# Moving the second set of modulation vectors from TensorE to VectorE, returning the memory of two tables, and new figures in the emitter of a two-layer diffusion backbone

## The chip, the cores and the metric

The kernel runs on one core of one Trainium2 chip. The metric is the device time of one execution in microseconds (us). Three executions of the kernel before took 1827.73, 1830.83 and 1835.16 us; their median is 1830.83 us. The profile shown here is of a further execution, of 1827.55 us.

## What is computed

The reference is a backbone of two layers over 2048 latent tokens of 1024 channels (x) with 256 context tokens. Both layers are modulated by vectors that come out of a conditioning vector c:

```python
s_lat = jax.nn.silu(c)
shift, scale, gate = jnp.split((s_lat @ ada_w[i] + ada_b[i])[:, None, :], 3, axis=-1)
a = rmsnorm(h, norm_g[i]) * (1.0 + scale) + shift
...
h = h + gate * y
```

Layer 0 (even) projects `a` to queries, keys, values, two gate paths and the input u of a state layer (S5: 32 groups of 16 channels, 64 complex states per group and direction, scanned forward and backward). Window attention (128 tokens to either side, 256 context tokens, a sink per head) and the state layer (followed by a gated linear unit, GLU) are joined by one output projection. Layer 1 (odd) is a pooling mixer: an input projection with gate, centred means over 3, 5, 9 and 17 tokens, a mixing matrix that is folded into the input weights, and an output projection. A final RMSNorm ends it.

For each layer `ada_w[i]` is 1024 by 3072. This text calls layer 0's shift and scale (for latents and context) the first set, and the other four vectors, layer 0's gate and layer 1's shift, scale and gate, the second set: 4096 sums of 1024 products each, 16.8 MB of weights. The second set is read for the first time by the output projection of layer 0.

## The kernel before, in words

Large products run on TensorE as three fp32r products of high and low halves (`split`, `products`), with the channel dimension on the partitions and 512 tokens as moving columns; smaller ones (state layer, tables, modulation) run on plain fp32 operands, for which the trace has two records per matmul.

**The emitter.** The program is not written in its final order. Each piece of work is a Python generator (`t_ada1`, `t_u`, `t_gen` and so on). An emitter (`Threads`) keeps a clock per engine from a cost for every instruction (`issue`, line 176; DMAs in `dma`, line 219), always resumes the generator whose next step is due first (`run`, line 243), and so writes one static order for each engine's queue. On the chip each engine works through its queue in that order and waits on semaphores; one SyncE queue issues all DMAs. The cost figures thus decide the order of all five queues, and for some elementwise steps (`lighter`, line 514) whether VectorE or GpSimd gets them. Bias terms hold back two of the generators.

**Memory.** All SBUF is given out by hand in words per partition (`Mem`, `Buf`, `Ring`): `core_f` of 16192 words and `x2` of 12384 words for fp32, `core_r` of 4096 and `x3` of 16384 for fp32r, and `x1` of 4128, which is reopened as fp32 or fp32r between stages. A generator that finds no room (`need`, line 404) waits until something is freed.

**Stages around the change.**
- *The u stage.* `t_load` loads x in five parts (the context, then quarters 2, 3, 0, 1) of eight rows of 128 channels, with at most 14 rows held. `t_stat`, `t_rstd`, `t_scale` and `t_apply` make the norm and the modulated, split rows; `rstd` (line 894) has two sets of small matmuls and a reciprocal (L492). `t_u` multiplies each quarter by four weight tiles for u (for the context also keys and values) and stores u to DRAM. Beside it run `t_s5par` (state parameters, GpSimd), then `t_etab` (four parts of a rotation table, stored to e_scr, in a work space `s5w` of 3328 words and `pw` of 512), `t_ltab` and `t_lags` (tables of the output side, stored to o_scr and r_scr).
- *The flag "x1f".* When `t_u` has ended, `t_main` takes six stage buffers of 512 words and two rope tables of 1024, reopens `x1` as fp32 and sets "x1f". The state layer waits for it: `t_s5u` and `t_s5e` (loads), `t_gen` (input tables, from PGr and PGi, two tables of 512 words), `t_s5` (input products), `t_rot` (rotation and scan, VectorE) and `t_s5out` (output products, z stored to z_scr). Beside it `t_main` runs the projection to keys, values, queries and gates (56 tiles of 24 products on TensorE).
- *Attention.* `t_qk` starts when the state layer has stored z and the gate stage is far enough; `t_exp`, `t_norm`, `t_pv` follow unit by unit (32 units), with `t_fold` and `t_glu` beside them.
- *Output projection of layer 0 (`t_out0`).* It waits for "fold" (the flag of `t_fold`), takes a weight stream (`Weights`: raw ring of 2 by 1024 words in `core_f`, split ring in `core_r`, which GLU holds until its end), then xin 3, hst 3, sqt 2 and r1 4 buffers of 512 words, all in `core_f`; then it waits for "gate0". Layer 1 follows.

**What the change touches.** `t_ada1` (lines 630 to 672) makes the second set. It starts when the first set has freed its buffers ("ada_free"), takes a ring of three buffers of 1024 words and a row buffer, and loads `adaM` in 32 loads of 512 KB. For each of eight blocks of 512 outputs it runs eight fp32 matmuls whose stationary operand is silu(c) (128 by 2) and whose moving operand is 512 columns of weights, copies the 2 by 512 result to SBUF (ScalarE), turns it onto partitions by four transposes of 2 by 128, and adds the bias on VectorE. It shares TensorE's queue with `t_u`.

`t_gen` (lines 1328 to 1353) frees PGr and PGi only if the flag "gen_end" already stands:

```python
        if "gen_end" in flags:
            PGr.free()
            PGi.free()
        flags.add("gen_end")
```

One `t_gen` runs in this kernel, so the flag never stands there, and the two tables are held to the end.

Helper lines of the profile: L464 `tt` (tensor_tensor), L475 `stt`, L483 `ttr` (tensor_tensor_reduce, a custom VectorE instruction and a read of its accumulator), L488 scan, L492 reciprocal, L498 `act`, L504 `mm`, L508 `transpose`, L512 `dma`. The name x_f stands for x1 or x2 opened as fp32, x_r for x1, x2 or x3 as fp32r.

Of the kernel before, what the change touches and what calls it, by code (L numbers as in the profile page):

```python
# [16 lines left out]
D = 1024  # L17
# [16 lines left out]
DMAF = 1.1  # L34
# [4 lines left out]
NADA1 = 3  # L39
# [78 lines left out]
class Threads:  # L118
# [8 lines left out]
    DMA_LAG, HOP, DELAY, CLOCK = 1.6, 0.1, 0.12, 3.4133  # L127

    def __init__(self):
        self.bias = {"t_fold": BF, "t_glu": BG}  # L130
        self.clock, self.spans, self.live, self.fresh = {}, {}, [], []
        self.now = self.end = self.stored = 0.0
        self.port = {"dve": [], "pool": []}
        self.lands = []
        self.window, self.busy, self.fast = 0, 0.0, False
# [40 lines left out]
    def issue(self, engine, cost, outs, ins, port=False):  # L176
# [29 lines left out]
        for x in outs:  # L206
            x[0] = f + self.HOP
        self.end = max(self.end, f)

# [9 lines left out]
    def dma(self, o, i, store):  # L219
# [10 lines left out]
        self.clock["dma"] = max(s + 0.5, self.clock.get("dma", 0.0)) + DMAF * n / run / 16 * (0.006 + run * 0.000194)  # L230
        f = self.clock["dma"] + self.DMA_LAG
        self.lands.append(max([f] + self.lands[-1:]))
# [57 lines left out]
def body(ctx: ExitStack, tc: tile.TileContext, I, out):  # L290
# [168 lines left out]
    def use(e, c, outs, *ins, port=False):  # L459
        th.issue(ename[id(e)], c, outs, [x for x in ins if isinstance(x, bass.AP)], port)  # L460
# [45 lines left out]
    def transpose(o, i, ident):  # L506
        use(TE, 0.22, [o], i)
        return TE.transpose(o, i, ident)  # L508
# [120 lines left out]

    def t_ada1():  # L630

        yield from wait("ada_free")
        ring = yield from need(lambda: Ring(NADA1, 2, 512))
        row = yield from need(lambda: Buf(512))
        w = {}

        def load(i):
            if i < 32:
                w[i] = ring.next()
                dma(w[i], I["adaM"][i // 4, i % 4].rearrange("p (k n) -> p k n", k=2))  # L640

        for i in range(NADA1):
            load(i)
        for blk in range(8):
            b = yield from get_bank()
            ps = bank(b)
            for i in range(4):
                yield from arrived(w[4 * blk + i])
                t_ = w.pop(4 * blk + i)
                for k in range(2):  # L650
                    mm(ps[0:2], silu.f[:, 2 * i + k], t_[:, k], i == k == 0, i == 3 and k == 1)
                yield
                load(4 * blk + i + NADA1)
            r = row.f[0:2]
            act(r, ps[0:2], AF.Copy, scale=0.5)
            yield
            for j in range(4):
                transpose(ps[:, 2 * j:2 * j + 2], r[:, 128 * j:128 * (j + 1)], K["ident"][0:2, 0:2])
            yield
            got = ps[:, 0:8:2]  # L660
            vec, sl = (gate0, sh1, gs1, gate1)[blk // 2], slice(4 * (blk % 2), 4 * (blk % 2) + 4)
            add = (K["b0"][:, 16:24], K["b1"][:, 0:8], K["b1"][:, 8:16], K["b1"][:, 16:24])[blk // 2]
            tt(V, vec[:, sl], got, add[:, sl], OP.add)
            put_bank(b)
            if blk // 2 == 2:
                stt(gs1[:, sl], gs1[:, sl], 1.0, K["g1"][:, sl], OP.add, OP.mult)
            if blk == 1:
                flags.add("gate0")
            yield
        flags.add("ada1")  # L670
        for b in (ring, row):
            b.free()
# [655 lines left out]
    def t_gen(e):  # L1328
# [20 lines left out]
        if "gen_end" in flags:  # L1349
            PGr.free()  # L1350
            PGi.free()
# [1232 lines left out]
def _layout(i):  # L2584
# [38 lines left out]
    def tiles(w):  # L2623
# [17 lines left out]
adaM=ac(np.concatenate([np.asarray(i["ada_w"][0])[:, 2 * D:], np.asarray(i["ada_w"][1])], axis=1)  # L2641
                .reshape(4, 2, 128, 8, 512).transpose(3, 0, 2, 1, 4).reshape(8, 4, 128, -1)),
# [26 lines left out]
```

## Time and profile before

| | before |
|---|---|
| median of three runs (lowest to highest) | 1830.83 us (1827.73 to 1835.16) |
| profiled execution, its own time | 1827.55 us |
| its span, first to last instruction | 1825.8 us |
| mean granted TensorE clock | 0.979 |
| busy: TensorE (PE), VectorE (DVE), ScalarE (ACT), GpSimd (POOL) | 1717.7, 1283.4, 828.3, 594.7 us |
| moved by DMA, mean rate | 286.16 MB, 157 GB/s |
| share of PE in the chain that ended last | 74% |

The profile is one execution, with times in us from the first instruction. "Busy" is the time in which an engine had an instruction in work. Windows give the busy time of each engine in a stretch, with the granted TensorE clock and the busy share of the 16 DMA engines. The chain of waits goes back from the last instruction to whatever released each step. A group line gives engine, line, operation, tiles, shape and count, then the busy time, the mean of one in ns, and the idle time of the engine just before, with what ended it.

### The profile page before, as it was taken

Reading aid. Unit: us, or ns where it says so; the run is one execution under the profiler, and the core shown is the slowest. Engines: PE = TensorE matmul, PEld = TensorE weight load, DVE = VectorE, ACT = ScalarE, POOL = GpSimd, SP = SyncE. Lnnn points to the kernel's source line nnn. Section 1 sums busy time; section 2 is a strip of 40 time slices with the busy share of each in tenths; the row PEclk is TensorE's granted clock in tenths of the full one; section 3 lists DMA queues with packets and bytes.
Section 4 is the critical chain, followed back from the end, with each engine's and each line's share of the span. In section 5 each row is a group of like instructions: output and inputs, shape, how many; then the busy total and the mean of one; then the engine's idle time right before and its main releaser. Section 6 shows DMA issues by size and latency. Waiting matters only on the chain.

```text
span 1825.8 us, 24990 instructions
## 1 busy us (share of the span) xinstructions
PE 1717.7 (94%) x8488; PEld 1366.8 (75%) x8488; DVE 1283.4 (70%) x2150; ACT 828.3 (45%) x1689; POOL 594.7 (33%) x722
## 2 busy tenths in 40 slices
PE   6899998979998999988897999999999999999997
PEld 1654465758887887777775788888888888888897
DVE  3569764997878945777888879687656764666634
ACT  4545431335444433687677766544322332222311
POOL 4887655663244410435363534230000000000000
PEclk9999998989998999999999999999999999999998
DMA  7777565235665456465855446687211263441332
GB/s 287 221 239 219 162 172 177 97 123 172 193 216 155 156 162 180 137 185 140 238 159 160 114 137 182 203 254 231 87 58 46 75 201 127 141 135 48 105 87 86
DMA packets 226000, 286.16 MB, mean 157 GB/s; under 512 B 60112, under 2 KB 155088, under 8 KB 224848
## 3 DMA queue, kind: packets, MB, share of 16 engines
q1 hardware_dynamic: 225872, 284.56, 51.6%
q8 instruction: 67, 1.10, 0.2%
q14 instruction: 61, 0.50, 0.1%
HBM read 204.60 MB, written 79.89 MB: 156 GB/s over the span
## 4 chain that ended last, share of the span: by engine, by line
PE 74%; DVE 9%; DMA 6%; ACT 4%; POOL 3%; issue 3%; SPq 1%; DVEq 0%; ACTq 0%; POOLq 0%
PE psum L504 71%; PE psum L508 3%; DVE x_r L464 2%; DVE core_f L464 2%; DVE x_f L464 2%; POOL core_f L464 2%; ACT x_f L498 2%; ACT x_r L498 1%; SPq L512 1%; POOL core_f L469 1%; DMA x_f<-u_scr 1%; DVE core_f L475 1%; DMA core_f<-a_scr 1%; DMA core_f<-sg_scr 1%; DMA core_f<-in_s5p 1%
## 5 line engine op out<-in xcount | busy, mean ns | idle before, releaser
L504 PE MATMUL psum<-x_r,core_r 128*128 128x512 f32 (+3 forms) x4536 | 1080.5, 393 | 5.7 <-ACT core_f L498 1.5
L504 PEld LDWEIGHTS psum<-x_r,core_r 128*128 128x128 f32 x4536 | 841.5, 189 | 199.1 <-issue 20.4
L504 PE MATMUL psum<-x_r 128*128 128x256 f32 (+3 forms) x1808 | 372.8, 348 | 13.7 <-DVE x_r L464 4.5
L464 DVE TENSOR_TENSOR core_f<-core_f 128x512 f32<-128x512 f32 (+20 forms) x443 | 301.3, 692 | 49.4 <-ACT core_f L498 22.0
L504 PEld LDWEIGHTS psum<-x_r 128*128 128x128 f32 x1808 | 284.0, 195 | 47.9 <-issue 12.9
L464 POOL TENSOR_TENSOR core_f<-core_f 128x32 f32<-128x32 f32 (+8 forms) x321 | 235.5, 748 | 178.9 <-ACT core_f L498 57.3
L464 DVE TENSOR_TENSOR core_r<-core_f,core_r 128x512 fp32r<-128x512 f32 (+1 forms) x182 | 135.1, 742 | 170.8 <-ACT core_r L498 168.1
L498 ACT ACTIVATE core_r<-core_f 128x512 fp32r<-128x512 f32 (+1 forms) x224 | 141.0, 632 | 220.6 <-PE psum L504 129.3
L498 ACT ACTIVATE core_f<-psum 128x512 f32<-128x512 f32 (+2 forms) x217 | 116.0, 535 | 257.9 <-PE psum L504 238.9
L498 ACT ACTIVATE x_r<-core_f 128x512 fp32r<-128x512 f32 (+5 forms) x173 | 127.0, 745 | 99.6 <-DVE core_f L475 69.0
L470 POOL TENSOR_SCALAR x_f<-x_f,core_f 128x640 f32<-128x640 f32 (+1 forms) x128 | 131.1, 1037 | 105.4 <-DVE core_f L492 66.7
L508 PE MATMUL psum<-core_f,x_f 128*128 128x128 f32 (+1 forms) x792 | 123.0, 279 | 30.5 <-DVE x_r L464 24.4
L464 DVE TENSOR_TENSOR x_r<-psum,x_r 128x512 fp32r<-128x512 f32 (+2 forms) x174 | 112.1, 649 | 48.9 <-ACT x_r L498 45.1
L508 PEld LDWEIGHTS psum<-core_f,x_f 128*128 128x128 f32 (+1 forms) x792 | 96.2, 144 | 62.8 <-DVE x_r L464 31.0
L498 ACT ACTIVATE x_f<-x_f,core_f 128x640 f32<-128x640 f32 (+2 forms) x155 | 123.5, 798 | 36.1 <-DVE core_f L475 32.4
L475 DVE SCALAR_TENSOR_TENSOR core_f<-core_f 128x512 f32<-128x512 f32 (+12 forms) x162 | 122.0, 762 | 20.8 <-DMA core_f<-h_scr 12.2
L498 ACT ACTIVATE core_f<-core_f 64x32 f32<-64x32 f32 (+7 forms) x224 | 83.4, 372 | 113.7 <-DVE core_f L475 94.9
L479 POOL COPY core_f<-core_f 128x16 f32<-128x16 f32 (+2 forms) x35 | 8.7, 262 | 369.1 <-DVE core_f L475 293.3
L464 POOL TENSOR_TENSOR core_r<-core_f,core_r 128x512 fp32r<-128x512 f32 x42 | 61.8, 1475 | 203.6 <-ACT core_r L498 203.6
L498 ACT ACTIVATE x_f<-psum 128x512 f32<-128x512 f32 (+5 forms) x187 | 77.7, 447 | 93.3 <-PE psum L504 80.7
L464 DVE TENSOR_TENSOR x_f<-x_f 128x512 f32<-128x512 f32 (+5 forms) x155 | 116.5, 780 | 3.4 <-ACT x_f L498 1.6
L498 ACT ACTIVATE x_r<-psum 128x512 fp32r<-128x512 f32 (+2 forms) x174 | 97.1, 562 | 48.1 <-PE psum L504 42.7
(64 smaller groups left out, 1314.0 us busy)
## 6 DMA issues: line engine op xcount, KB each, us to landing
core_f<-in_wo SPq DMA_DIRECT2D x48, 512.0 KB
core_f<-in_w SPq DMA_DIRECT2D x42, 512.0 KB
x_f<-in_adaM SPq DMA_DIRECT2D x32, 512.0 KB
core_f<-in_xT SPq DMA_DIRECT2D x45, 256.0 KB
x_f<-in_adaN SPq DMA_DIRECT2D x8, 1024.0 KB
o_scr<-core_f SPq DMA_DIRECT2D x32, 256.0 KB
x_f<-o_scr SPq DMA_DIRECT2D x16, 512.0 KB
sg_scr<-core_f SPq DMA_DIRECT2D x32, 256.0 KB
```

Source lines behind the costliest of these rows:

```text
L464: return e.tensor_tensor(o, a, b, op=op)
L469: return e.tensor_scalar(o, a, s1, None, op0=op0)
L470: return e.tensor_scalar(o, a, s1, s2, op0=op0, op1=op1)
L475: return V.scalar_tensor_tensor(o, a, s, b, op0=op0, op1=op1)
L479: return e.tensor_copy(o, a)
L498: return S.activation(o, i, f, **kw)
L504: return TE.matmul(o, w, x, start=start, stop=stop)
L508: return TE.transpose(o, i, ident)
L512: return nc.sync.dma_start(o, i)
```

## The change

The diff has three parts.

1. `t_ada1` is rewritten. It now waits for "x1f". It takes a buffer of 1024 words with silu(c) on every partition (c is loaded once with a partition broadcast, and ScalarE and VectorE make its silu) and a ring of three rows of 1024 words. The weights come transposed (`adaT`, 4096 rows of 1024): each of 32 loads of 512 KB brings 128 outputs onto the partitions, and one `ttr` of 128 by 1024 on VectorE multiplies them by silu(c) and sums along the row into one column of `ada`, a new buffer of 32 words that is kept to the end. Its order is gate0, shift1, scale1, gate1; the bias additions follow ("gate0" after eight rows, "ada1" at the end). TensorE, PSUM and the transposes are no longer used.
2. `t_gen` frees PGr and PGi at its end, without a condition: 1024 words of `core_f`.
3. The emitter's figures: a transpose costs 0.11 instead of 0.22; a result of TensorE is ready 0.17 later (DRAIN); the clocks of VectorE, ScalarE and GpSimd stand 0.08, 0.095 and 0.035 before the end of their last instruction (AHEAD); and DMA time is kept on 16 rings by the number of rings that a transfer's shape uses, with new constants, where it was one clock, and transfers may land out of order.

```diff
-DMAF = 1.1
+DMAF = 1.0
...
-NADA1 = 3
...
-    DMA_LAG, HOP, DELAY, CLOCK = 1.6, 0.1, 0.12, 3.4133
+    DMA_LAG, HOP, DELAY, CLOCK, DRAIN = 1.6, 0.1, 0.12, 3.4133, 0.17
+    AHEAD = {"dve": 0.08, "act": 0.095, "pool": 0.035}
...
-        self.lands = []
+        self.lands, self.rings = [], [0.0] * 16
...
-            x[0] = f + self.HOP
+            x[0] = f + self.HOP + (self.DRAIN if engine == "pe" else 0.0)
         self.end = max(self.end, f)
+        self.clock[engine] = f - self.AHEAD.get(engine, 0.0)
...
-        self.clock["dma"] = max(s + 0.5, self.clock.get("dma", 0.0)) + DMAF * n / run / 16 * (0.006 + run * 0.000194)
+        a, b = (next((int(d[1]) for d in x.ap if int(d[1]) > 1), 1) for x in (o, i))
+        k = max(k for k in range(1, 17) if a % k == b % k == 0)
+        for j in range(k):
+            self.rings[j] = max(s + 0.5, self.rings[j]) + n / run / k * (0.008 + run * 0.000152 * DMAF)
+        self.clock["dma"] = max(self.rings[:k])
         f = self.clock["dma"] + self.DMA_LAG
-        self.lands.append(max([f] + self.lands[-1:]))
+        self.lands.append(f)
...
     def transpose(o, i, ident):
-        use(TE, 0.22, [o], i)
+        use(TE, 0.11, [o], i)
...
+    ada = Buf(32, top=True)
+
     def t_ada1():
 
-        yield from wait("ada_free")
-        ring = yield from need(lambda: Ring(NADA1, 2, 512))
-        row = yield from need(lambda: Buf(512))
+        yield from wait("x1f")
+        silu_c = yield from need(lambda: Buf(D))
+        ring = yield from need(lambda: Ring(3, D))
+        dma(silu_c.f, I["c"].partition_broadcast(128))
         w = {}
 
         def load(i):
             if i < 32:
                 w[i] = ring.next()
-                dma(w[i], I["adaM"][i // 4, i % 4].rearrange("p (k n) -> p k n", k=2))
...
+                dma(w[i], I["adaT"][128 * i:128 * (i + 1), :])
+
+        yield LOAD
+        t_ = ring.next()
+        act(t_, silu_c.f, AF.Tanh, scale=0.5)
+        yield
+        stt(silu_c.f, t_, 1.0, silu_c.f, OP.add, OP.mult)
+        load(0)
+        load(1)
+        for i in range(32):
+            load(i + 2)
+            yield from arrived(w[i])
+            x = w.pop(i)
+            ttr(x, x, silu_c.f, OP.mult, OP.add, 0.0, ada.f[:, i:i + 1], scale=0.5)
+            yield
+            if i == 7:
+                tt(V, gate0, ada.f[:, 0:8], K["b0"][:, 16:24], OP.add)
                 flags.add("gate0")
...
         flags.add("ada1")
-        for b in (ring, row):
+        yield
+        for b in (ring, silu_c):
             b.free()
...
-        if "gen_end" in flags:
-            PGr.free()
-            PGi.free()
+        PGr.free()
+        PGi.free()
         flags.add("gen_end")
```

More of the change, by code (lines that the diff above doesn't have):

```diff
@@ L639, in load @@
                 w[i] = ring.next()
-                dma(w[i], I["adaM"][i // 4, i % 4].rearrange("p (k n) -> p k n", k=2))
[L642 to L655, printed above, removed]
-            yield
[L657 to L667, printed above, removed]
+                dma(w[i], I["adaT"][128 * i:128 * (i + 1), :])
[11 more added lines that the diff above has]
+            ttr(x, x, silu_c.f, OP.mult, OP.add, 0.0, ada.f[:, i:i + 1], scale=0.5)
+            yield
+            if i == 7:
+                tt(V, gate0, ada.f[:, 0:8], K["b0"][:, 16:24], OP.add)
                 flags.add("gate0")
-            yield
+        tt(V, sh1, ada.f[:, 8:16], K["b1"][:, 0:8], OP.add)
+        tt(V, gs1, ada.f[:, 16:24], K["b1"][:, 8:16], OP.add)
+        stt(gs1, gs1, 1.0, K["g1"], OP.add, OP.mult)
+        tt(V, gate1, ada.f[:, 24:32], K["b1"][:, 16:24], OP.add)
         flags.add("ada1")
-        for b in (ring, row):
+        yield
+        for b in (ring, silu_c):
             b.free()
@@ L2640, in _layout @@
         adaN=ac(np.asarray(i["ada_w"][0])[:, :2 * D].reshape(8, 128, 2, 4, 256).transpose(3, 1, 0, 2, 4).reshape(4, 128, -1)),
-adaM=ac(np.concatenate([np.asarray(i["ada_w"][0])[:, 2 * D:], np.asarray(i["ada_w"][1])], axis=1)
-                .reshape(4, 2, 128, 8, 512).transpose(3, 0, 2, 1, 4).reshape(8, 4, 128, -1)),
+adaT=ac(np.concatenate([np.asarray(i["ada_w"][0])[:, 2 * D:].T, np.asarray(i["ada_w"][1]).T])),
         w0=tiles(np.asarray(i["even_w_in"][0])[:, order]),
```

## The prediction

> **What bounds the kernel now.** I read the page first, then the engines' busy time by stage, TensorE's order of work in the u stage, and last who waits for whom. The page and the windows (columns: window, its length, then busy us and count for PE, PEld, DVE, ACT and POOL, granted clock, DMA share, GB/s):
>
> ```profile
> span 1825.8 us, 24990 instructions
> ...
> PE 1717.7 (94%) x8488; PEld 1366.8 (75%) x8488; DVE 1283.4 (70%) x2150; ACT 828.3 (45%) x1689; POOL 594.7 (33%) x722
> ```
> ```profile
> 50.00:130.00 80.00, 74.04 (x338) 46.35 (x338) 43.66 (x73) 43.57 (x71) 70.73 (x165) 0.98 0.77 241
> 130.00:260.00 130.00, 126.52 (x464) 64.60 (x463) 106.48 (x160) 59.02 (x131) 81.67 (x97) 1.00 0.61 175
> 260.00:311.00 51.00, 42.64 (x162) 30.59 (x163) 23.24 (x33) 8.91 (x27) 32.25 (x46) 0.90 0.61 187
> 311.00:400.00 89.00, 75.41 (x355) 56.11 (x354) 80.37 (x107) 28.07 (x82) 58.14 (x48) 0.94 0.30 100
> 400.00:664.00 264.00, 254.90 (x1475) 222.18 (x1473) 216.31 (x342) 123.51 (x278) 98.96 (x74) 0.98 0.58 176
> 664.00:757.00 93.00, 90.42 (x446) 74.91 (x445) 52.65 (x122) 44.72 (x97) 13.99 (x15) 1.00 0.54 159
> 757.00:950.00 193.00, 170.40 (x969) 143.97 (x968) 156.72 (x293) 141.42 (x297) 91.44 (x74) 0.95 0.66 183
> 950.00:1025.00 75.00, 59.57 (x331) 47.09 (x330) 64.18 (x141) 55.21 (x125) 35.44 (x37) 0.93 0.51 137
> 1025.00:1175.00 150.00, 148.49 (x804) 125.12 (x804) 117.94 (x240) 98.30 (x208) 56.07 (x52) 1.00 0.55 165
> 1175.00:1800.00 625.00, 625.00 (x2937) 531.35 (x2936) 389.43 (x553) 200.24 (x328) 31.49 (x48) 1.00 0.40 123
> ```
>
> TensorE bounds the kernel: 1717.7 of 1825.8 us, and from 1025 to 1800 it is idle for 1.5 us. So a saving counts if it takes work from TensorE's queue where that queue is the limit, or fills one of its gaps. Between 50 and 1175 the gaps come to 82.6 us; the largest for its length is 950 to 1025, 15.4 of 75 us. VectorE is the second engine: 106.5 of 130 us late in the u stage, 80.4 of 89 us at the start of the state layer.
>
> **What is removed from TensorE.** The group of the old matmuls (with the first set's), the loads, and TensorE in order of time (start, length, what; in brackets the idle time before):
>
> ```profile
> L504 PE MATMUL psum<-x_f,core_f 128*2 128x512 f32 x192 | 90.2, 602 | 2.8 <-DMA x_f<-in_adaM 1.6 <-DMA x_f<-in_adaN 1.2
> ```
> ```profile
> L512 SPq DMA_DIRECT2D x_f<-in_adaM x32: 327/382/737, 52.1 to 223.2; - x32
> ```
> ```profile
> 203.47 1.88 PE L504 MATMUL psum<-x_f,core_f 128*2 128x512 f32 x4
> 205.28 1.65 PE L504 MATMUL psum<-x_r,core_r 128*128 128x512 f32 x6
> ...
> 211.30 0.41 PE L508 MATMUL psum<-core_f,x_f 2*128 2x2 f32 x4
> 211.64 1.65 PE L504 MATMUL psum<-x_r,core_r 128*128 128x512 f32 x6
> ...
> 214.27 7.13 PE L504 MATMUL psum<-x_r,core_r 128*128 128x512 f32 x30
> ...
> 226.89 0.96 PE L504 MATMUL psum<-x_r,core_r 128*128 128x512 f32 x3
> ...
> 238.27 0.50 PE L504 MATMUL psum<-x_r,core_r 128*128 128x512 f32 x1 [0.95 <-ACT x_r L498]
> 239.00 1.18 PE L504 MATMUL psum<-x_r,core_r 128*128 128x512 f32 x4 [0.23 <-DVE x_r L464]
> ```
>
> The 192 records are two per matmul: 32 matmuls of the first set, 64 of the second. One of the 32 loads feeds two matmuls, four records, and holds TensorE from 203.47 to 205.28, 1.81 us: 32 x 1.81 = 57.9 us. The eight times four transposes hold it from 211.30 to 211.64 each, 8 x 0.34 = 2.7 us. So **60.6 us** leave TensorE's queue, all between 52 and 237 us, where it is busy for 200.6 of 210 us (50 to 260).
>
> How much of that shortens the u stage? At most 60.6 us, if TensorE alone sets its end. The last quarter says that it doesn't:
>
> ```profile
> L512 SPq DMA_DIRECT2D x_f<-in_xT x19: 328/384/1447, 27.7 to 159.4; - x19
> ```
> ```profile
> 188.41 0.17 DVE L492 RECIPROCAL x_f<-x_f 128x4 f32<-128x4 f32 x1
> ```
> ```profile
> ACT x_f L498 <- PE psum L504: 24.0, 12, 3.5
> ```
>
> The last row of x is requested at 159.4, its quarter's norm is at the reciprocal at 188.4, and TensorE takes the rows one at a time (three records each: the 226.89 row) until 238.3, when it waits for ScalarE and VectorE. The other tiles of that quarter need 4 x 24 products x 0.238 us (7.13 us for 30) = 22.8 us in all. So from 159 to 239 rows are made hardly faster than they are used. TensorE enters this chain through the matmuls of the norm, which queue behind modulation and u products (between 128 and 240 ScalarE's work on x_f alone waits 24.0 us for TensorE), and by its own pace before. If only the norm's queueing goes, some 10 us are won; if all, 60.6. I take **30 us**, half: before about 170 us TensorE does not wait for rows, after it does. The end of the u stage, and "x1f" with it, comes near 230 instead of 260.
>
> A price here is the clock. At 84% busy (260 to 311) the granted clock is 0.90; the thinner u stage would be like that. Its products left, some 100 us, would take up to 11 us more, most of it inside waits; I take +2. [...]
>
> **What is added to VectorE.** No row shows a `ttr` of 128x1024 from SBUF. Near rows:
>
> ```profile
> L483 DVE DVE_READ_ACCUMULATOR2_ANT core_f<- x144: 71/82/92, 709.3 to 1142.3; 128x1 f32 x144
> L483 DVE CUSTOM_DVE_ANT_0 x_f<-psum,x_f x128: 392/815/826, 708.9 to 1141.5; 128x640 f32<-128x640 f32 x112, 128x256 f32<-128x256 f32 x16
> ```
> ```profile
> L464 DVE TENSOR_TENSOR core_f<-core_f 128x1024 f32<-128x1024 f32 x8 | 16.1, 2045 | 8.4 <-POOL core_f L464 8.4
> L464 DVE TENSOR_TENSOR core_f<-core_f 128x1016 f32<-128x1016 f32 x8 | 9.7, 1217 | 0.3
> ```
>
> Two SBUF operands of 128x1016 cost 1217 ns in layer 1, where GpSimd is nearly idle, and 2045 ns at 128x1024 in the output projection's inputs, where it isn't. With 82 ns for the accumulator, 32 rows cost 41.6 to 68.1 us. In the state layer GpSimd is busy for 37% (99.0 of 264 us), so I take 1.22 + 0.37 x 0.83 + 0.08 = 1.61 us, **51 us** in all. [...]
>
> When does this run? Memory decides. Words left at "x1f": the state layer's rings take nearly all of x1 and x2. In the trace its first input transpose comes only when the last rotation table has been stored and the work space `s5w` and `pw`, 3840 words, is back:
>
> ```profile
> L512 SPq DMA_DIRECT2D e_scr<-core_f x16: 513/626/1149, 177.0 to 315.9; - x16
> ```
> ```profile
> L508 PE MATMUL psum<-core_f,x_f x16: 269/272/328, 323.8 to 337.1; 128*128 128x128 f32 x16
> ```
> ```profile
> L512 SPq DMA_DIRECT2D r_scr<-core_f x68: 302/410/996, 154.8 to 405.2; - x68
> L512 SPq DMA_DIRECT2D z_scr<-x_f x64: 565/576/762, 413.5 to 664.6; - x64
> ```
>
> `t_gen` stands before `t_ada1` in the list and takes its 1536 words; the new 1024 and 3 x 1024 then don't fit until the lag tables end (last r_scr store at 405.2). So the 32 instructions fall at about 400 to 490, into the state layer's 82% (216.3 of 264). VectorE has 80.4 + 216.3 = 296.7 us of work from 311 to 664; with 51 more, at the 90% that it shows from 311 to 400, 348 / 0.90 = 387 us instead of 353: 34 us more. Its start, tied to the rotation tables, moves perhaps 8 us forward. z ends near **690** instead of 664.
>
> What covers that? Before, TensorE has gate-stage work from 664 to the first attention result at 708.9 (the L483 row), 45 us. The gate stage now runs 30 us earlier, so attention's other condition is met near 679, and the gate stage's last eight tiles (8 x 24 x 0.238 = 46 us) bridge the 21 us until attention starts near 700. They are missing later as cover, where TensorE is 88% busy (170.4 of 193): 21 x 0.12 = 2.5 us; I take **+5**, bounds 0 and 30.
>
> The 16.8 MB move from a DMA share of 0.77 and 0.61 to one of 0.58; 32 SyncE issues (0.38 us each, 12 us) move too, past the state layer's loads. I take nothing for these, with the price in the rivals. Of the rest of `t_ada1`, eight copies leave ScalarE and one tanh comes, and ten small additions on VectorE become five: nothing, ScalarE is busy for less than half of these windows.
>
> **The returned tables.** The first weights of the output projection are requested, and its first result is stored:
>
> ```profile
> L512 SPq DMA_DIRECT2D core_f<-in_wo x48: 327/333/1538, 961.2 to 1726.1; - x48
> ```
> ```profile
> L512 SPq DMA_DIRECT2D h_scr<-core_f x48: 319/332/467, 1044.2 to 1542.1; - x48
> ```
>
> 83 us lie between, for a tile of 5.7 us. Adding up `core_f` at that point (constants 584, the two tables 1024, weight stream 2048, mixing rows 4096, attention's 96, 1024 and 1536, xin, hst, sqt and two of the four r1 buffers 5120) gives 15528 of 16192: 664 are free, two times 512 are missing. With the tables back, less `ada`'s 32, 1656 are. The projection can then start right after GLU and fill TensorE in 950 to 1025: 15.4 us idle, of which I take **-12**. If the free words lie in pieces, 0.
>
> **The emitter's figures** reorder everything by a little. They can touch the 82.6 us of gaps, either way; I take 0, bounds -15 and +15.
>
> Sum: -30 + 2 + 5 - 12 = -35. The profiled execution took 1827.55 us (span 1825.8), 3.3 below the median of 1830.83; 1827.55 - 35 = **1792 us**.
>
> **Rivals.** *TensorE alone sets the u stage.* All 60.6 us count: 1827.55 - 60.6 + 7 - 12 = 1762 us. For it: 200.6 of 210 us busy. Against: the waits at 238. Chance 0.16.
>
> *Nothing moves.* The rows of the last quarters set the u stage (10 us won), the later state layer costs 10, the free words are in pieces: about 1827 us. For it: the 188 to 239 rows, VectorE at 82%. Against: before 170 TensorE waits for nothing. Chance 0.09.
>
> *Slower: VectorE waits for weight rows.* The `ttr` stand in one in-order queue with rotation and scan; behind each late row the whole state layer waits. The ring is three rows deep, and 512 KB at the 176 GB/s shown there are 3.0 us, twice the 1.61 us that a row takes on VectorE. At 2 us of waiting a row the state layer ends 64 us later still, near 755, attention starts near 765, and the gate stage, at 757 before, is used up near 727: 40 us or more idle on TensorE, and as much again when `t_rot` and the row loads block SyncE: 1827.55 - 40 + 70 = 1858 us. It decides from about 1 us a row. Against: in the u stage TensorE waited 1.6 us for 32 such rows in all. Chance 0.08.
>
> **How the numbers follow.** Forecast (u stage 15 to 45 us shorter): 0.67, 1770 to 1815 with the emitter's bounds. With the first rival's lower half and the no-change case the range is 1745 to 1826. A change of 0.5%, 9 us, is about what a measurement can tell here: faster 0.83, same 0.09, slower 0.08.
>
> **What would show it.** PE busy near 1657; the u stage's end (last u_scr store) near 230; first `ttr` after the last r_scr store, 1.2 to 2.0 us each; last z_scr store near 690 - 8 to 30 either way; first h_scr store soon after GLU, TensorE over 95% busy in the 75 us after it. Wrong if the u stage ends at 250 or later, if `ttr` run beside the u stage or wait for DMA, or if PE's gaps grow by more than 40 us.

## The result, and the profile after

The kernel after takes 1811.15 us (median of 4 runs, 1808.19 to 1811.88), the kernel before 1830.67 beside it: a ratio of 0.9885, 95% interval 0.9866 to 0.9905, or 19.5 us less. The forecast was 1792, so direction and range held, and about half of the forecast gain is missing. The profiled execution of after took 1811.88 us, 15.7 less than the profiled one of before; the stages below add up to that.

The head of after's page. TensorE has 52.2 us less work and 36.5 us more idle time (span less busy: 108.1 before, 144.6 now):

```profile
span 1810.1 us, 24680 instructions
...
PE 1665.5 (92%) x8328; PEld 1363.3 (75%) x8328; DVE 1325.3 (73%) x2222; ACT 823.0 (45%) x1682; POOL 603.2 (33%) x710
```

The windows of after (columns as in the prediction):

```profile
50.00:130.00 80.00, 63.28 (x319) 53.48 (x318) 47.73 (x81) 48.48 (x80) 72.99 (x168) 0.87 0.51 154
130.00:225.00 95.00, 81.08 (x307) 54.38 (x307) 83.80 (x121) 44.85 (x100) 57.31 (x70) 0.89 0.38 101
225.00:313.00 88.00, 85.22 (x352) 62.90 (x351) 66.96 (x106) 20.05 (x60) 47.05 (x59) 0.98 0.57 184
...
378.00:560.00 182.00, 158.58 (x857) 135.24 (x856) 169.14 (x241) 71.51 (x159) 96.77 (x68) 0.93 0.76 251
560.00:695.00 135.00, 130.08 (x762) 112.60 (x763) 107.54 (x182) 67.06 (x154) 45.19 (x36) 1.00 0.60 181
...
727.00:950.00 223.00, 189.07 (x1088) 158.58 (x1087) 182.16 (x353) 161.62 (x348) 106.38 (x87) 0.95 0.62 175
950.00:1025.00 75.00, 71.92 (x386) 60.38 (x385) 61.19 (x126) 51.70 (x112) 26.25 (x23) 0.98 0.58 170
1025.00:1188.00 163.00, 158.78 (x859) 133.31 (x858) 127.17 (x263) 107.08 (x228) 65.23 (x58) 1.00 0.54 167
1188.00:1260.00 72.00, 66.06 (x283) 52.13 (x282) 56.12 (x86) 33.97 (x57) 10.37 (x7) 0.93 0.70 232
```

The kernel before, in those windows that the prediction did not cut there:

```profile
225.00:313.00 88.00, 77.78 (x295) 51.17 (x295) 49.81 (x76) 25.25 (x64) 51.05 (x69) 0.94 0.60 178
...
378.00:560.00 182.00, 170.03 (x990) 146.38 (x988) 154.35 (x236) 89.92 (x206) 73.13 (x58) 0.98 0.59 180
560.00:695.00 135.00, 131.14 (x698) 112.89 (x698) 95.16 (x152) 52.21 (x112) 40.88 (x29) 0.97 0.53 160
...
727.00:950.00 223.00, 200.40 (x1134) 169.82 (x1133) 178.42 (x348) 161.30 (x342) 103.41 (x87) 0.95 0.61 172
...
1025.00:1188.00 163.00, 161.49 (x861) 135.90 (x861) 127.46 (x255) 105.31 (x221) 56.07 (x52) 1.00 0.58 173
```

Length less busy time is TensorE's idle time, and its change places the 36.5 us: 1.0 before 50 us; 15.6 from 50 to 313; 0.7 from 313 to 378; 11.4 from 378 to 560; 0.1 up to 727; 11.3 from 727 to 950; **-12.3** from 950 to 1025; 8.7 from 1025 to 1260; nothing behind that.

Single tiles and lines, each with count, shortest, median and longest ns, and the first and last start. First the last stores of u before, then after in order: u stage, the second set on VectorE, the state layer's output, attention, and the output projection's first weights and results:

```profile
L512 SPq DMA_DIRECT2D u_scr<-core_f x24: 302/453/1221, 54.6 to 265.3; - x24
```
```profile
L517 SPq DMA_DIRECT2D u_scr<-x_f x88: 303/448/1280, 66.2 to 230.7; - x88
...
L488 DVE CUSTOM_DVE_ANT_0 core_f<-core_f x32: 1209/1219/2312, 391.1 to 550.7; 128x1024 f32<-128x1024 f32 x32
...
L517 SPq DMA_DIRECT2D z_scr<-core_f x48: 571/581/972, 423.9 to 694.2; - x48
...
L488 DVE DVE_READ_ACCUMULATOR2_ANT core_f<- x176: 72/83/94, 392.2 to 1158.7; 128x1 f32 x176
L488 DVE CUSTOM_DVE_ANT_0 x_f<-psum,x_f x128: 408/815/826, 704.4 to 1157.9; 128x640 f32<-128x640 f32 x112, 128x256 f32<-128x256 f32 x16
...
L517 SPq DMA_DIRECT2D core_f<-in_wo x48: 327/333/558, 945.1 to 1710.3; - x48
...
L517 SPq DMA_DIRECT2D h_scr<-core_f x48: 319/333/711, 967.8 to 1526.5; - x48
```

The landmarks came where they were forecast: end of the u stage 230.7 (230), rows from 391 (about 400), last z 694.2 (690), attention 704.4 (700), first h 967.8, 23 us after the first weights. And yet half the gain is missing. So it was lost between the landmarks, and the runs had to say where.

### The profile page after: what moved, and what is told of

Read it like the earlier page. It is cut to its first block, busy times and chain, and to the rows that moved or that the text cites. A ratio compares the mean times of both kernels' runs of the same rounds, so it can differ in the third digit from the quotient of the medians.

```text
span 1810.1 us, 24680 instructions
## 1 busy us (share of the span) xinstructions
PE 1665.5 (92%) x8328; PEld 1363.3 (75%) x8328; DVE 1325.3 (73%) x2222; ACT 823.0 (45%) x1682; POOL 603.2 (33%) x710
## 4 chain that ended last, share of the span: by engine, by line
PE 53%; DMA 4%; DVE 3%; ACT 2%; issue 1%; SPq 1%; POOL 0%; DVEq 0%; ACTq 0%; POOLq 0%
PE psum L509 50%; PE psum L513 3%; ACT x_r L503 1%; DVE x_r L469 1%; SPq L517 1%; ACT x_f L503 1%; DVE core_f L469 1%; DVE core_f L480 1%; DMA core_f<-sg_scr 1%; DMA core_f<-att_scr 0%; DMA core_f<-k_scr 0%; DVE x_f L488 0%; DMA core_f<-h_scr 0%; ACT core_f L503 0%; DMA core_f<-in_wo 0%
## 5 line engine op out<-in xcount | busy, mean ns | idle before, releaser
L509 PE MATMUL psum<-x_r,core_r 128*128 128x512 f32 (+3 forms) x4536 | 1094.4, 395 | 20.1 <-POOL x_r L469 7.2
L509 PE MATMUL psum<-x_r 128*128 128x256 f32 (+3 forms) x1808 | 369.3, 348 | 15.6 <-ACT core_f L503 7.8
L469 DVE TENSOR_TENSOR core_f<-core_f 128x512 f32<-128x512 f32 (+18 forms) x452 | 298.0, 670 | 41.1 <-ACT core_f L503 16.0
L469 POOL TENSOR_TENSOR core_f<-core_f 128x32 f32<-128x32 f32 (+7 forms) x314 | 237.5, 769 | 196.0 <-DVE core_f L469 66.4
L469 DVE TENSOR_TENSOR core_r<-core_f,core_r 128x512 fp32r<-128x512 f32 (+1 forms) x186 | 144.6, 778 | 157.4 <-ACT core_r L503 155.2
L475 POOL TENSOR_SCALAR x_f<-x_f,core_f 128x640 f32<-128x640 f32 (+1 forms) x128 | 142.7, 1127 | 150.8 <-DVE core_f L497 38.3
L509 PE MATMUL psum<-x_f 128*128 128x128 f32 (+2 forms) x896 | 143.4, 309 | 23.5 <-ACT x_f L503 7.6
L509 PEld LDWEIGHTS psum<-x_f 128*128 128x128 f32 (+1 forms) x896 | 114.2, 190 | 48.9 <-issue 11.7
L503 ACT ACTIVATE core_f<-core_f 128x512 f32<-128x512 f32 (+7 forms) x151 | 71.4, 473 | 165.7 <-DVE core_f L480 152.0
L503 ACT ACTIVATE x_f<-psum 128x512 f32<-128x512 f32 (+6 forms) x191 | 80.3, 453 | 144.7 <-PE psum L509 129.6
L480 DVE SCALAR_TENSOR_TENSOR core_f<-core_f 128x512 f32<-128x512 f32 (+13 forms) x162 | 117.6, 737 | 14.2 <-DMA core_f<-h_scr 9.0
L469 DVE TENSOR_TENSOR x_f<-x_f 128x512 f32<-128x512 f32 (+5 forms) x151 | 118.1, 812 | 10.2 <-POOL x_f L469 5.6
L513 PE MATMUL psum<-core_f,x_f 128*128 128x128 f32 (+1 forms) x632 | 98.4, 278 | 27.1 <-DVE x_r L469 24.7
```

The source lines that it names most:

```text
L469: return e.tensor_tensor(o, a, b, op=op)
L475: return e.tensor_scalar(o, a, s1, s2, op0=op0, op1=op1)
L480: return V.scalar_tensor_tensor(o, a, s, b, op0=op0, op1=op1)
L503: return S.activation(o, i, f, **kw)
L509: return TE.matmul(o, w, x, start=start, stop=stop)
```

## The experiments

The theory at the start (A): the u stage gives its gain, and the 32 instructions on VectorE give much of it back by making the state layer late. The rivals: the gain comes from the figures (B), or the figures cost what is missing (C). All medians below stand beside a kernel before of 1830.9 to 1831.3 us. Only the work and the times of `ada_only`, `rows_early` and the two versions with old figures at the end are used here, not what they compute; each has the 8328 matmul records of after and its 32 row instructions.

### One part alone, one part undone

`ada_only` is before with the new `t_ada1`; figures old, tables held:

> The kernel before with the new t_ada1 alone (old figures, tables not returned). Theory A (the removed TensorE work shortens the u stage by some 30 us, the state layer then ends some 30 us later because of the 48 us of tensor_tensor_reduce, and attention starts at nearly the old time): u stage ends near 225 to 235, attention starts at 700 to 712, total 1815 to 1828 us, some 5 to 10 us under before. Theory B (the gain of the changed kernel comes from the new figures, and moving the modulation is worth nothing or less): 1831 us or more. Theory C (the new figures cost what is missing to the forecast): 1800 or less even without the tables.

`figures_only` is before with all new figures:

> The kernel before with the new figures alone. Theory A: within 6 us of before, 1825 to 1837 us, since TensorE's queue holds the same work. Theory B: 1810 to 1820 us. Theory C: 1840 us or more, with TensorE's gaps between 50 and 1175 grown from 82.6 us to over 95.

`no_tables` is after with

```
-        PGr.free()
-        PGi.free()
         flags.add("gen_end")
```

> The changed kernel with the two tables held to the end. Theory A (the returned 1024 words let the output projection of layer 0 start right after GLU): its first h_scr store moves back from 968 to some 70 us later, TensorE is idle again for about 15 of the 75 us after GLU, total 1818 to 1825 us. Rival: the early start only delays attention and is worth nothing: 1809 to 1813 us.

`no_second_set` is after without loads, `silu(c)` and the 32 instructions:

```
...
-        for i in range(32):
...
+        V.memset(ada.f, 0.0)
+        tt(V, gate0, ada.f[:, 0:8], K["b0"][:, 16:24], OP.add)
+        flags.add("gate0")
```

> The changed kernel without the second set's products: gate, shift and scale are made from the biases alone, so 32 loads, 32 tensor_tensor_reduce and silu(c) are left out. Theory A: the state layer ends 25 to 40 us earlier (last z_scr store 655 to 670 instead of 694), attention starts at 665 to 685 instead of 704, total 1775 to 1792 us. Rival (the new order of the queues, not VectorE's added work, holds the state layer): last z_scr store within 10 us of 694, total 1800 us or more.

`old_second_set` is after with the old `t_ada1`, so tables and figures without the move:

> The kernel after with the second set put back onto TensorE, as in the kernel before; the returned tables and the new figures stay. The new figures alone took 1846.9, and the returned tables were worth 4.9 us beside the new second set. Theory (the tables' memory lets the output projection start early, and what it fills is mostly given back at attention's end): total 1838 to 1846, output projection's first store near 980. Rival (the 15 us of gap before 1025 are won in full): 1828 to 1834. If it comes out near 1811, the second set's move is worth nothing and the tables with the figures make the gain.

| second set | figures | tables | kernel | us | ratio, 95% interval |
|---|---|---|---|---|---|
| TensorE | old | held | before | 1830.67 | 1 |
| VectorE | old | held | ada_only | 1835.21 | 1.0026, 1.0008 to 1.0044 |
| TensorE | new | held | figures_only | 1846.85 | 1.0086, 1.0071 to 1.0101 |
| VectorE | new | held | no_tables | 1816.03 | 0.9916, 0.9900 to 0.9932 |
| TensorE | new | returned | old_second_set | 1855.06 | 1.0137, 1.0114 to 1.0160 |
| VectorE | new | returned | after | 1811.15 | 0.9885, 0.9866 to 0.9905 |
| left out | new | returned | no_second_set | 1792.20 | 0.9789, 0.9774 to 0.9803 |

The parts do not add. Moving the second set costs 4.5 us with the old figures (1.5 to 8 by the interval) and gains 30.8 with the new ones (44 with the tables returned too). The new figures cost 16 alone and gain 19 beside the move. Returned tables gain 4.9 beside the move and cost 8.2 without it. So B is out as an account by itself, and C too; A holds in that leaving the set out gives 19 us more. Several times missed what was expected: `ada_only` lies in B's range, with attention at 737.4 where A had 700 to 712; `figures_only` lies in C's, with gaps of TensorE of 89.6 us from 50 to 1175 where C had over 95; `no_tables` falls between its two sides; `old_second_set` is above both.

Why do the figures alone cost? The keys' loads and the state layer's output show it, here in `figures_only`:

```profile
L518 SPq DMA_DIRECT2D core_f<-k_scr x36: 444/587/3691, 714.1 to 1013.9; - x36
L518 SPq DMA_DIRECT2D z_scr<-x_f x64: 565/580/627, 406.3 to 636.9; - x64
```

and the same loads before and after:

```profile
L512 SPq DMA_DIRECT2D core_f<-k_scr x36: 450/587/3017, 689.8 to 1002.6; - x36
```
```profile
L517 SPq DMA_DIRECT2D core_f<-k_scr x36: 444/566/712, 661.4 to 990.3; - x36
```

In 13 of the 14 kernels attention starts 10 to 12 us after the last z or 19 to 23 us after the first keys are requested, whichever is later (`rows_after_z`, below, is the exception, with 14 after z). Before: 689.8 + 19.1 = 708.9 with z at 664.6. `figures_only`: z is 28 us earlier, 636.9, and attention 26.5 us *later*, at 735.4, since the keys are requested only at 714.1; they take 7168 words that the gate stage's third quarter holds. After: z at 694.2 + 10.2 = 704.4 with keys at 661.4. `ada_only`: z at 725.8, attention at 737.4. Two conditions, and each edit moves another one; an earlier z was worth nothing where keys were late.

### Is it VectorE's time, or the rows themselves?

`no_second_set` leaves out loads and work together. `short_rows` keeps the loads and cuts the work:

```
-            ttr(x, x, silu_c.f, OP.mult, OP.add, 0.0, ada.f[:, i:i + 1], scale=0.5)
+            ttr(x[:, 0:8], x[:, 0:8], silu_c.f[:, 0:8], OP.mult, OP.add, 0.0, ada.f[:, i:i + 1], scale=0.5)
```

> The kernel after with each of the 32 instructions cut to 8 of its 1024 columns: the 32 loads, their requests on SyncE, the waits and the order of the kernel stay, and VectorE loses about 32 x 1.3 = 42 us of work in the state layer (the sums of the second set are left incomplete). Without the whole second set the time was 1792.2, with it 1811.2. Theory (VectorE's time is the price): last z_scr store 655 to 675, attention's first result at most 685, total 1792 to 1800. Rival (the 16.8 MB of rows and their requests are the price, through the DMA queues and SyncE): last z_scr store at 685 or later, total 1805 to 1812.

1823.70 us (ratio 0.9962, 0.9948 to 0.9976): slower than after, with less work in it. Neither side expected that. Its z, keys, attention, and its windows:

```profile
L517 SPq DMA_DIRECT2D z_scr<-core_f x48: 571/579/1117, 407.1 to 659.8; - x48
L517 SPq DMA_DIRECT2D core_f<-k_scr x36: 445/587/3470, 664.7 to 979.3; - x36
L488 DVE CUSTOM_DVE_ANT_0 x_f<-psum,x_f x128: 395/814/996, 687.4 to 1148.3; 128x640 f32<-128x640 f32 x112, 128x256 f32<-128x256 f32 x16
```
```profile
378.00:560.00 182.00, 164.09 (x940) 142.03 (x939) 153.81 (x297) 81.14 (x184) 65.86 (x53) 0.95 0.79 265
560.00:655.00 95.00, 88.33 (x518) 77.29 (x517) 72.97 (x124) 42.25 (x96) 25.99 (x19) 0.98 0.50 158
...
1188.00:1300.00 112.00, 96.74 (x385) 75.03 (x384) 73.42 (x120) 41.35 (x68) 4.79 (x5) 0.85 0.54 168
```

The same of `no_second_set`, its windows cut at its own landmarks (attention from 664.8):

```profile
L517 SPq DMA_DIRECT2D z_scr<-core_f x48: 568/577/927, 402.7 to 652.6; - x48
L517 SPq DMA_DIRECT2D core_f<-k_scr x36: 450/587/4098, 631.2 to 955.6; - x36
```
```profile
372.00:560.00 188.00, 178.42 (x1054) 155.15 (x1053) 167.65 (x252) 87.22 (x196) 75.26 (x59) 1.00 0.58 183
560.00:655.00 95.00, 95.00 (x552) 82.27 (x551) 69.21 (x132) 48.50 (x111) 14.19 (x12) 1.00 0.60 182
```

Of the 41.6 us by which z comes earlier without the second set (694.2 to 652.6), 34.4 are there with VectorE's instructions cut (659.8 in `short_rows`), about the 33 us of work that the cut takes from VectorE between 378 and 560: there A is right. `short_rows` is not after with less work and all else equal, though: the emitter prices the short instruction lower and plans anew (2247 instructions on VectorE and 685 on GpSimd, in after 2222 and 710).

TensorE's idle time in the state layer follows VectorE's work only in part. It is 28.3 us in after (23.4 + 4.9), 24.6 in `short_rows` (17.9 + 6.7), 15.8 before and 9.6 in `no_second_set`. In after and in `short_rows` it goes to different waits. Of after's 28.3 us the profile puts 12.9 down to VectorE, 7.6 to ScalarE, 5.2 to GpSimd and 2.6 to the state layer's own loads of u; of the 24.6 in `short_rows` it puts 10.6 down to those loads and 5.3 to VectorE. In `no_second_set` the loads of u make 3.7. Their rows in after (378 to 695) and `short_rows` (378 to 655), us in total, times, longest:

```profile
PE psum L509 <- DMA x_f<-u_scr: 2.6, 3, 1.3
```
```profile
PE psum L509 <- DMA x_f<-u_scr: 10.6, 4, 6.7
```

With the instructions cut, the 32 rows are requested in 122 us where after takes 151, the DMA share is 0.79, and SyncE, whose queue issues the loads of u too, waits for row loads for 11.9 us from 378 to 560; in after for 1.9. The row of `short_rows`:

```profile
SPq L517 <- DMA core_f<-in_adaT: 11.9, 13, 2.2
```

So where VectorE's work goes, waits for loads take its place, and the keys (664.7, against 631.2 without the set) stay late. That fits that the earlier z bought little. It does not explain the 12.5 us that were lost on top. In the last window TensorE is idle for 15.3 us (1188 to 1300), 5.9 in after, and runs at a granted clock of 0.85.

### Memory behind GLU

The stream that prepares the normed input of layer 1 (the texts here call it the MLP's input) shows its start by its first reciprocal after 1186: in `short_rows` at 1215.6, in after at 1193.9. It needs 528 and 1024 words, and the keys' buffers give some back, and the extra mixing rows (`NMORE`, 512 words each) may have taken what lies beside. Two edits of one figure test that, one in each direction. The figure also sets how many buffers the mixing has, so they do not part the words from the mixing's own pace.

`short_one_more`: `short_rows` with `NMORE = 1` in place of 2.

> The kernel with the 32 instructions cut to 8 columns (1823.7, the sums left incomplete), and the two extra rows that the mixing takes at the end of GLU made one. There the last z came 34 us earlier than in the kernel after and the output projection ended 3.8 us earlier, yet the end came 8.8 us later: the stream that prepares the MLP's input started at 1212 in place of 1191, when the mixing had ended, and TensorE then stood idle for 12 us at 1197 to 1209 and 1273 to 1279 and ran at a granted clock of 0.89. Theory (its memory, 528 and 1024 words, was taken by the extra mixing rows): the stream starts at 1175 to 1195, the output projection ends near 1256 as before, total 1808 to 1814. Rival (it is late for another reason, its data or its place in the order): 1820 to 1826.

`after_three_more`: after with `NMORE = 3`.

> The kernel after with three extra mixing rows in place of two, taken at the end of GLU. Nothing before GLU's end (936) changes. Theory (memory between GLU and the output projection's end is a limit of its own, which the kernel after keeps by little): the stream that prepares the MLP's input starts at 1209 or later in place of 1191, TensorE's gaps from 1190 to 1290 grow by 8 to 13 us, total 1819 to 1826. Rival (that stage has slack; the end is set by attention's start alone): 1808 to 1814.

They gave 1809.34 (0.9890, 0.9872 to 0.9907) and 1824.74 (0.9968, 0.9956 to 0.9980): 14.4 us won by one buffer less, 13.6 lost by one more. Reciprocals and window of `short_one_more`, of `after_three_more`, and of after:

```profile
L497 DVE RECIPROCAL core_f<-core_f x3: 178/178/180, 1192.5 to 1268.4; 128x4 f32<-128x4 f32 x3
```
```profile
1188.00:1300.00 112.00, 103.36 (x447) 81.97 (x446) 80.70 (x125) 46.65 (x76) 10.53 (x9) 0.92 0.56 176
```
```profile
L497 DVE RECIPROCAL core_f<-core_f x3: 178/179/179, 1219.7 to 1286.9; 128x4 f32<-128x4 f32 x3
```
```profile
1188.00:1300.00 112.00, 103.32 (x423) 81.53 (x422) 75.20 (x123) 45.58 (x75) 6.23 (x6) 0.89 0.58 183
```
```profile
L497 DVE RECIPROCAL core_f<-core_f x3: 171/178/179, 1193.9 to 1275.3; 128x4 f32<-128x4 f32 x3
```
```profile
1188.00:1300.00 112.00, 106.06 (x467) 85.45 (x466) 83.17 (x128) 48.56 (x80) 10.99 (x10) 0.95 0.56 186
```

The start moves as the theory has it, by 23 and 26 us, and the time with it. TensorE's idle time in the window moves by only 6.6 and 2.7 us, where the theory for `after_three_more` had 8 to 13; the granted clock does much of the rest: 0.92 - 0.85 over 112 us are an estimated 7.8 us, with 6.6 some 14, and 0.95 - 0.89 are 6.7, with 2.7 some 9. The profiled executions are 11.1 and 12.9 us apart, so these sums close to about 3 us and no better. This stage has a limit of its own, which after keeps by little.

With that out of the way, `short_one_more` is the kernel after without some 35 us on VectorE (45.8 to 11.2 from 378 to 560) and with one extra mixing row fewer, which was not tried alone, and takes 1.8 us less. So cutting VectorE's work while the loads stay bought next to nothing. The other 17 us up to `no_second_set` go with what is still there: the loads, their requests, the 4096 words that rows and silu(c) hold, and the order that follows. This is no clean split. In after TensorE's waits are put down mostly to VectorE, ScalarE and GpSimd, and no run has the row instructions without the loads, so what they would cost then is open.

### Other places for the rows

`rows_after_z` leaves rows 0 to 7 and starts the other 24 when the state layer has ended; `rows_early` puts `t_ada1` ahead of the rotation tables:

```
...
+        yield from wait("z")
+        yield from rows1(8, 32)
...
```

> The kernel after with rows 0 to 7 (the gate that the output projection needs) where they were, and rows 8 to 31 started only when the last z is made, beside attention's start; silu(c) is made twice. Theory (the rows cost time because VectorE sets the state layer's end, which attention waits for): last z_scr store 660 to 672, attention's first result 670 to 690; the rows then stand in attention's part, where VectorE is busy for 182 of 223 us, and cost there again, but less: total 1798 to 1808. Rival (it is VectorE's work as such that counts between 311 and 950, wherever it stands): 1809 or more, with GLU's end near 936 as before.

```
-        th.run([... t_w0(), t_etab(), t_s5u(), ...
+        th.run([... t_w0(), t_etab(), t_ada1(), t_s5u(), ...
```

> The kernel after with the second set's rows ahead of the rotation tables in the list of streams, so that they take the memory first when the u stage ends, at about 225 to 420. Theory (what counts is when the state layer ends): the rotation tables start later by the time that the rows hold their memory, some 40 to 50 us, the state layer ends at 700 to 725 and the total is 1813 to 1830. Rival (there is room on VectorE between 225 and 313, where it is busy for 67 of 88 us, and the state layer is free of the rows): last z_scr store 660 to 685, total 1792 to 1805.

1817.37 (0.9929, 0.9914 to 0.9944) and 1847.13 us (1.0088, 1.0061 to 1.0116). In `rows_after_z` the last z is at 668.0, 26 us earlier, and attention starts 22 us earlier, at 682.1; but the rows now stand in attention's part, the first h store comes at 984.5 in place of 967.8, and the time is the rival's. Whether it is VectorE's time that counts there, as the rival has it, or the 24 loads that moved along, was not separated; and the first weights of the output projection, which follow GLU's end, are requested 19 us later than in after, where the rival had no change. In `rows_early` the time is 17 us above the theory's range. The last z is at 722.0: the rotation tables begin as before and are stored 24 us later (last e_scr store 340.4, in after 316.6), and the state layer's first input transposes come at 387.9 in place of 321.7. Neither beats after, and no version with the whole second set does.

### Which figures

`after_old_engine_figures` takes back the engines' leads, the delay behind TensorE and the transpose; `after_old_dma_figures` takes back the sixteen rings.

```
...
-        self.clock[engine] = f - self.AHEAD.get(engine, 0.0)
...
-        use(TE, 0.11, [o], i)
+        use(TE, 0.22, [o], i)
...
```

> The kernel after with the engines' old figures (no lead of 0.08, 0.095 and 0.035 us on VectorE, ScalarE and GpSimd, no 0.17 us behind TensorE's results, a transpose at 0.22); the figures of the DMA rings stay new. The new figures were worth 19.2 us beside the new second set (1835.2 with the old, 1816.0 with the new, tables held in both). Theory (they act through the order on VectorE in the state layer, where the rows, rotation and scan compete): last z_scr store at 715 to 730 in place of 694, total 1825 to 1838. Rival (the gain is the DMA rings'): last z_scr store at 690 to 700, total 1808 to 1816.

```
...
-        for j in range(k):
-            self.rings[j] = max(s + 0.5, self.rings[j]) + n / run / k * (0.008 + run * 0.000152 * DMAF)
+        self.clock["dma"] = max(s + 0.5, self.clock.get("dma", 0.0)) + DMAF * n / run / 16 * (0.006 + run * 0.000194)
...
```

> The kernel after with the old figures for DMA (one common queue of 1.1 times 0.000194 us a byte in place of sixteen rings, arrival in order); the engines' figures stay new. Theory (the engines' figures carry the gain): last z_scr store at 690 to 705, total 1808 to 1818. Rival (the rings carry it): last z_scr store at 710 or later, total 1822 to 1838.

1874.99 (1.0256, 1.0237 to 1.0276) and 1818.13 us (0.9943, 0.9928 to 0.9959): the rings are worth 7 us here, the engines' figures 64, far more than theory or rival had. VectorE's waits from 378 to 600 in `after_old_engine_figures`, then in after from 378 to 560 (us in total, times, longest):

```profile
DVE core_f L467 <- DMA core_f<-in_adaT: 12.9, 5, 5.4
DVE core_f L486 <- DMA core_f<-in_adaT: 12.4, 5, 6.3
```
```profile
DVE core_f L488 <- DMA core_f<-in_adaT: 0.7, 1, 0.7
```

25.3 us of waiting are put down to weight rows against 0.7, with the same instructions in another order; 12.4 stand before the row instructions themselves, 12.9 before others. The last z comes at 742.8. `ada_only`, which has the old figures too, shows 14.8 us of such waits (14.5 before other instructions), and `after_old_dma_figures`, with the new engines' figures, 0.4. That is the prediction's third rival, in a version of this kernel: 0.8 us a row, near the 1 us from which it was said to decide, and a time of 1875 where 1858 had been worked out for 2 us a row. Its condition was met there and not in after, and the engines' figures decided it. Part of the 64 us lies in later stages, where this version also idles (11.4 us from 1025 to 1188, 4.2 in after); that share was not tried by itself.

## Why the prediction was right, and where it fell short

**Right.** 60.6 us of matmuls left TensorE, and part of them became idle time because the u stage has a second limit: the stage ended 34.6 us earlier (last u store 265.3, now 230.7; the prediction had 260 to 230) where 30 were taken. TensorE's busy time fell by 52.2 us, so by difference 8.4 went to slower matmuls, in the windows at 0.87 and 0.89 among others; the stage from 50 to 225 holds 144.4 us of work where about 200.6 - 60.6 = 140.0 were left. The +2 for the clock was low, and its direction right. In shorter windows of after the granted clock is half or full:

```profile
115.00:120.00 5.00, 4.53 (x15) 3.95 (x16) 2.19 (x8) 1.24 (x3) 4.37 (x18) 0.50 0.54 198
...
155.00:160.00 5.00, 3.71 (x13) 2.39 (x12) 4.80 (x9) 0.39 (x1) 4.77 (x8) 0.50 0.32 109
```

From 165 to 170 it is 1.00. In windows of 1 us, but for those on an edge, the clock from 50 to 225 is 0.50 in six stretches (about 56 to 63, 84 to 87, 111 to 121, 148 to 162, 193 to 196 and 203 to 206, some 41 us) and 1.00 between them, so 0.87 and 0.89 are means over stretches at half and at full clock. The products follow it: 15 of them take 3.56 us from 140.46 on, 0.24 us each at 1.00, and 7 of the same form take 3.33 from 117.19 on, 0.48 each at 0.50. The half clock at 111 sets in inside a wait of 9.7 us (105.7 to 115.5); around 155 it is at half too, though no wait from 140 to 170 is over 2.1 us. So the length of the wait alone does not say here when the clock falls.

Right too are the price of the new instructions, 45.6 us and 2.5 for their accumulators against 51, their place, and with both the state layer's end within 4 us.

**The first step that failed is the +5 for cover.** It had TensorE pay only for the gate stage's tiles that are missing beside attention, 21 us at 12% idle. TensorE's idle time rose by 11.4 us inside the state layer (378 to 560) and by 11.3 beside attention (727 to 950): 23 in place of 5, within the bound of 30. The first figure the step did not have at all. The second is its own mechanism, at four times the 2.5 worked out: the gate stage is used up 34 us sooner (its last store at 730.6 in place of 764.5), and attention without it is a chain. What TensorE waits for there, after and before (from 757):

```profile
PE psum L513 <- DVE x_r L469: 20.6, 15, 5.0
```
```profile
PE psum L508 <- DVE x_r L464: 11.6, 10, 2.6
```

An average idle share of 12% was the wrong price for taking away the very work that filled it.

**The second is "I take nothing for these"**, for 16.8 MB of rows and 32 requests moved past the state layer's loads. The price stood only in a rival, as VectorE waiting, and in after VectorE does not wait (0.7 us). But with VectorE's work cut and the loads kept (`short_one_more`) the kernel is still 17 us above the one without the set. What those 17 us are made of is open: DMA share, SyncE's queue, the words held and the order were not separated, and in after itself TensorE waits more for VectorE's results than for loads.

**The third is the -12 of the tables.** The gap from 950 to 1025 closed by 12.3 us, as worked out. But 8.7 us opened behind it. In `no_tables` attention ends at 1118.2 and TensorE idles 0.5 us from 1025 to 1158:

```profile
L488 DVE DVE_READ_ACCUMULATOR2_ANT core_f<- x176: 73/82/98, 393.0 to 1118.2; 128x1 f32 x176
```
```profile
1025.00:1158.00 133.00, 132.49 (x715) 111.90 (x714) 105.23 (x216) 87.05 (x184) 50.15 (x46) 1.00 0.55 167
```

In after attention ends at 1158.7, 40 us later, beside the projection, which fits that the two share TensorE; and from 1150 to 1300 TensorE waits 5.9 us for ScalarE and GpSimd. The projection's first store comes 70 us earlier than in `no_tables` (967.8 against 1037.9), its last only 7 (1260.8 against 1267.9). 4.9 us are left, of which the intervals leave the size open by some 4.

**The fourth is 0 for the figures**, bounds 15 either way: 16 alone, -19 beside the move, both beyond the bounds. The order is no small term here, since it chooses which of two conditions attention waits for.

Together: -60.6 + 8.4 of slower work + 16.6 of idle time up to 313, 23.5 from there to 950, -12.3 + 8.7 behind it, which is -15.7, the difference of the profiled executions. Against the prediction's terms: up to 313 it is -35.6 where -28 was forecast, from there to 950 it is 23.5 where 5 was, and behind it -3.6 where -12 was. The u stage gave 7.6 us more than was taken, which no step had worked out, and paid for some of what the cover and the tables cost. Without that luck the time would be an estimated 1819, above the 1815 of the forecast's main case.

## What to carry to other kernels

Landmarks that come where they were forecast do not make the time: work that moves off the busiest engine also takes away what filled the gaps of the next stage, so price the next stage by its chain without that filler, not by its average idle share. A limit that is cut can show another one behind it: with VectorE's work cut, TensorE waited for loads instead, so equal idle time is not the same wait. And where an emitter plans the order and the memory, one buffer more or less moved the time by 14 us here, so the time of a version with a part left out is believed only after its landmarks have been read.

## What the runs showed of the hardware

The 32 instructions take 1209 ns at least and 1219 in the median, but up to 2312. Cut to 8 columns (`short_rows`) they take 168 in the median and up to 1310. The longest of each in order of time (start, length, engine), with what GpSimd does beside it; first after, then `short_rows`:

```profile
514.07 1.74 POOL L469 TENSOR_TENSOR core_r<-core_f,core_r 128x512 fp32r<-128x512 f32 x1
514.58 2.31 DVE L488 CUSTOM_DVE_ANT_0 core_f<-core_f 128x1024 f32<-128x1024 f32 x1
```
```profile
411.17 1.31 POOL L469 TENSOR_TENSOR x_f<-x_f 128x512 f32<-128x512 f32 x1 [6.14 <-DVE x_f L493]
411.20 1.31 DVE L488 CUSTOM_DVE_ANT_0 core_f<-core_f 128x8 f32<-128x8 f32 x1
```

The excess over the median is 1.09 and 1.14 us whether 1024 or 8 columns are read, and it is what is left of GpSimd's instruction: 514.07 + 1.74 = 515.81, and a median length of 1.22 us from there ends at 517.03; the record ends at 516.89; in `short_rows` 411.17 + 1.31 = 412.48, and the record ends at 412.51. So VectorE's instruction there lasts as if it had waited for the rest of the other one. The rows of after bear that out: 11 of the 32 take 1.39 to 2.31 us, each of them starts while a GpSimd instruction is running, and each ends 1.07 to 1.09 us after that one's end; the other 21 take 1.21 to 1.23 us, and 20 of them start with none running (the one at 427.89 starts 0.06 us before one ends). In one more pair it is also the later one that takes longer: the row of after that starts at 413.12 takes 1.21 us, and GpSimd's instruction that starts at 413.51 takes 1.95, where the same kind takes 1.29 from 538.22 on. The estimate of 1.61 us a row, which took the wait from GpSimd's busy share, came out a little above the measured mean of 1424 + 78 ns.
